# Ten in-projection tiles of a hybrid decoder layer over 516 of 528 positions

## The chip, the cores and the metric

One NeuronCore of a Trainium2 chip runs the whole layer in one launch. The metric is the device time of a launch in microseconds; smaller is better. The engines are named as in the profile: PE is TensorE's matmuls and PEld its weight loads, DVE is VectorE, ACT is ScalarE, POOL is GpSimd, SP is the queue that issues most DMAs.

## The reference

The layer puts 16 learned positions ahead of 512 tokens (528 positions, width 2048, float32), runs a mixer and a feed-forward block, and returns the 512 token positions. The part that matters here:

```python
n = rmsnorm(h, g_pre_mix)                 # (528, 2048)
z = n @ w_in                              # conv: B, C, h (1024 each); rwkv: r, k, v (1024 each), wd, ad (96 each), gd (256)
y_conv = B * causal_dwconv(C * h, conv_w) # kernel of 3 positions
zr = zr + (shift_by_one(zr) - zr) * mu    # token shift of all rwkv columns
r, k, v, wd, ad, gd = split(zr)
log_w = -DECAY_SCALE * sigmoid(w0 + tanh(wd) @ w_decay_up)
a = sigmoid(a0 + ad @ a_up)
g = sigmoid(gd) @ g_up
# S_t = S_{t-1} diag(w_t) + (S_{t-1} a_t) b_t^T + v_t k_t^T ;  y_t = S_t r_t
...
y_rwkv = (group_norm(y) + sum(r * k * r_k) * v) * g
h = h + rmsnorm(concat(y_conv, y_rwkv) @ w_out)
h = h + rmsnorm(conv_glu(rmsnorm(h)))     # conv over 3 positions in the gate
return h[16:]
```

k, v and the decays of a position enter the state and so reach all later positions. r and g of a position enter that position's own output alone. The feed-forward block's convolution looks back two positions, so the mixer's output is needed from position 14 on, and r and g from there, with z one position earlier for the shift.

## The kernel before, in words

Activations lie with channels on the 128 partitions and positions along the free axis. Every large product is done as three products of float32r parts: an operand is split into a rounded part `hi` and a remainder `lo`, and hi*hi, hi*lo and lo*hi are summed in PSUM. A tile of the in-projection is 128 output channels; `inproj` runs `gemm` for it, 16 steps of k (four loads of weights with four steps each), three products, and two halves of the positions, since a PSUM bank holds 512 values: 96 matmuls, each with its own weight load. The halves of the positions are given as a tuple: `HL` is (0, 264), (264, 528), and `HC`, used for two of the three convolution tiles of each group, is (12, 270), (270, 528); `T0` is 14.

There are 52 such tiles: 4 of the LoRAs (decay, a, and two of the gate, called `T_GD` on), 8 each of k, r and v, and 24 for the convolution. `lora_in` does the LoRA's tiles, `rkv(P)` the k, r and v tiles of head pair P, `conv(j)` the convolution's. For an rwkv tile `shifted` calls `inproj` and then `shift`: `evac` multiplies PSUM by the norm's factor into the tile `z` (DVE), ACT copies z times mu into `zm` one position later, with a zero ahead (a POOL memset of one column), and DVE mixes z * (1 - mu) + zm into the output tile (`k`, `r`, `v`, or `tb` for LoRA's). The tail of r, k and v, 16 columns that fill the last chunk of 32 positions, is cleared by a POOL memset ahead of the matmuls.

Head pairs then go through `prep` (which reads r on POOL into `XR`, and on DVE for the bonus), `inverse`, and `scan`, 17 chunks of 32 positions in sequence for each of four groups of four heads; `norm` and, for the last two pairs, `head_norm` finish them. The last pair's output is called `k` again, and its scratch tile `lo` is shared with the product that the last convolution group stores to `ysp`.

The stage is written as generators. A loop of its own time model decides in which order their steps are taken: scans, preps and norms take the steps that are due, and the in-projection tiles fill what is left (k, r, v of the pairs first, then the convolution). The list that results is not yet the order on the engines. `Plan` keeps all operations of the stage with their dependencies, gives each a cost by shape (`Plan.time`; for a matmul below it is n / 2400 + 0.0115 us for n columns), simulates the engines, tries eight rankings and emits the one with the shortest simulated span:

```python
            return max(0.222, n / 600 + 0.004) if x["args"][1].tile.dtype is F32 else n / 2400 + 0.0115
```

In-projection matmuls have the rank `FILL`: PE takes them where nothing else is ready. Each engine's queue then runs in that order. The out-projection follows, first two tiles outside a plan, then the rest and the feed-forward block by Strassen-like sums, under plans of their own. All instructions go through one recording helper, so the profile gives line 231 for them, and tiles' names tell them apart.

Of the kernel before, what the change touches and what calls it, by code (L numbers as in the profile page):

```python
# [12 lines left out]
AF = mybir.ActivationFunctionType  # L13
ALU = mybir.AluOpType
# [7 lines left out]
L = SEQ + META  # L22
# [6 lines left out]
T0 = META - 2  # L29
# [481 lines left out]
def hymba(tc, I, out, ysp=None):  # L511
    nc = tc.nc
    plan = Plan(tc)
    V, S, G, PE, SP = (Engine(plan, n, e) for n, e in (("DVE", nc.vector), ("ACT", nc.scalar), ("POOL", nc.gpsimd),
                                                       ("PE", nc.tensor), ("SP", nc.sync)))
# [19 lines left out]
    def pc(n, i):  # L535
        c = COLS[n] + i
        return par[0][:, c:c + 1] if c < NMIX else par[1][:, c - NMIX:c - NMIX + 1]
# [14 lines left out]
    def gemm(src, mov, spans, first=None, into=None, kept=None, parts=1):  # L552


        for ku in range(KT // 4):
            if kept is not None:
                hi, lo = kept[ku]
            else:
                hi, lo = wload(src[ku], into and into[ku]) if ku or first is None else first
            for k4 in range(4):  # L560
                k = ku * 4 + k4
                ws = slice(k4 * 128, k4 * 128 + 128)
                xh, xl = mov[k]
                for pi, (w, x) in enumerate(((hi, xh), (hi, xl), (lo, xh))):
                    for o, a, b in spans:
                        PE.matmul(o, w[:, ws], x[:, a:b], start=(k == 0 and pi == 0),
                                  stop=(k == KT - 1 and pi == 2))
                    if pi == 2 or parts == 3:
                        yield
# [16 lines left out]
    def split(x, hi, lo, scale=None):  # L586
        if scale is None:
            S.copy(hi, x)
            V.tensor_tensor(out=lo, in0=x, in1=hi.bitcast(F32), op=ALU.subtract)
        else:  # L590
            S.activation(out=hi, in_=x, func=AF.Copy, scale=scale)
            V.scalar_tensor_tensor(out=lo, in0=x, scalar=scale, in1=hi.bitcast(F32), op0=ALU.mult, op1=ALU.subtract)
# [31 lines left out]
    HL = ((0, 264), (264, 528))  # L624
# [3 lines left out]
    with ExitStack() as ctx1:  # L628
# [3 lines left out]
        omu = p1.tile([128, 28 + NP], F32, name="omu")  # L632
# [4 lines left out]
        for i in range(3):  # L637
            t = p1.tile([128, 2, 2, 64], F32, name=f"SUV{i}")
# [9 lines left out]
        for k in range(KT):  # L648
# [3 lines left out]
            if k == 1:  # L652
                SP.dma_start(par[0][:, KT:], I["par"][:, KT:NMIX])
                V.tensor_scalar(out=omu[:, :28], in0=par[0][:, COLS["mu"]:COLS["mu"] + 28], scalar1=-1.0, scalar2=1.0,
                                op0=ALU.mult, op1=ALU.add)
                V.tensor_scalar(out=omu[:, 28:], in0=par[0][:, COLS["k_a"]:COLS["k_a"] + NP], scalar1=-1.0, scalar2=1.0,
                                op0=ALU.mult, op1=ALU.add)
# [20 lines left out]
        def inproj(t, halves, into=None):  # L678
            if t == T_K:

                ps = [stp.tile([128, 512], F32, name="st") for _ in range(2)]
            else:
                ps = mp.tile([128, 2, 512], F32, name="mps")
            yield from gemm(I["w_in"][t], xs, [((ps[i] if isinstance(ps, list) else ps[:, i])[:, :b - a], a, b)
                                               for i, (a, b) in enumerate(halves)],
                            first if t == 0 else None, into, None, 1 if t in (T_WD, T_AD) else PARTS)
            return ps

        def evac(ps, t0, o, halves):

            rstd = norm1[0]
            with plan.step(0.6):
                if not isinstance(ps, list) and halves[0][1] - halves[0][0] == halves[1][1] - halves[1][0]:
                    n = halves[0][1] - halves[0][0]
                    a = halves[0][0]
                    V.tensor_tensor(out=o[:, a - t0:a - t0 + 2 * n].rearrange("p (a b) -> p a b", a=2),
                                    in0=ps[:, :, :n], in1=rstd[:, a:a + 2 * n].rearrange("p (a b) -> p a b", a=2),
                                    op=ALU.mult)
                else:
                    for i, (a, b) in enumerate(halves):  # L700
                        x = ps[i] if isinstance(ps, list) else ps[:, i]
                        V.tensor_tensor(out=o[:, a - t0:b - t0], in0=x[:, :b - a], in1=rstd[:, a:b], op=ALU.mult)

        def shift(ps, mi, o):
            z = p1.tile([128, L], F32, name="z", bufs=2)
            evac(ps, 0, z, HL)
            zm = p1.tile([128, L + 1], F32, name="zm")
            G.memset(zm[:, 0:1], 0.0)
            S.activation(out=zm[:, 1:], in_=z, func=AF.Copy, scale=pc("mu", mi))
            V.scalar_tensor_tensor(out=o, in0=z, scalar=omu[:, mi:mi + 1], in1=zm[:, :L], op0=ALU.mult, op1=ALU.add)  # L710

        def shifted(t, o):
            shift((yield from inproj(t, HL)), t, o)

        blkr = p1.tile([128, 128], F32R, name="blkr")
        blk = p1.tile([128, L], F32, name="lo")[:, :128]
        SP.dma_start(blk, I["cst"][:, 128:256])
# [24 lines left out]
        def lora_in(t):  # L742
            if t == T_WD:
                wad = p1.tile(xr_shape, F32R, name="XR", bufs=2).rearrange("r c a p h t -> r (c a p h t)")
                wd, ad = inproj(t, HL), inproj(T_AD, HL, [
                    (wad[:, 1024 * i:1024 * i + 512], wad[:, 1024 * i + 512:1024 * i + 1024]) for i in range(KT // 4)])
                for _ in range(KT):
                    next(wd)
                    yield
                    if _ >= LAG:  # L750
                        next(ad)
                        yield
                for _ in range(max(0, LAG - LATE)):
                    next(ad)
                    yield
                ps0 = yield from wd
                rstd = p1.tile([128, L], F32, name="rstd")
                m, q = p1.tile([128, LP], F32, name="t1"), p1.tile([128, LP], F32, name="t2")
                for a, b in HL:
                    rms([x[:, a:b] for x in ss], rstd[:, a:b], m[:, a:b], q[:, a:b], aux, "aux")  # L760
                norm1.append(rstd)
                both = p1.tile(xr_shape, F32R, name="XR", bufs=2).rearrange("r c a p h t -> r (c a p h t)")
                lox.extend([both[:, i * L:i * L + L] for i in (2 * n, 2 * n + 1)] for n in range(4))
                tb = p1.tile([128, 2 * C * C + C], F32, name="tb")
                o = tb[:, :L]
                shift(ps0, t, o)
                S.activation(out=o, in_=o, func=AF.Tanh)
                split(o, *lox[0])
                o = tb[:, L:2 * L]
                shift((yield from ad), T_AD, o)  # L770
                split(o, *lox[1])
            else:
                o = p1.tile([128, 2 * C * C + C], F32, name="tb")[:, :L]
                yield from shifted(t, o)
                S.activation(out=o, in_=o, func=AF.Sigmoid)
                split(o, *lox[2 + t - T_GD])

# [34 lines left out]
        def rkv(P):  # L812
            for nm, T in (("k", T_K), ("r", T_R), ("v", T_V)):
                o = p1.tile([128, LP], F32, name=nm, bufs=2)
                G.memset(o[:, L:], 0.0)
                yield from shifted(T + P, o[:, :L])
                st[nm, P] = o

        def prep(P):
# [325 lines left out]
                SP.dma_start(ysp[NP + P], o)  # L1145

        ylast = {}
        HC = ((T0 - 2, T0 - 2 + 258), (T0 + 256, L))

        def conv(j):  # L1150
            zc = p1.tile([128, TY + 2], F32, name="zm")
            evac((yield from inproj(T_CC + j, HC)), T0 - 2, zc, HC)
            zh = p1.tile([128, TY + 2], F32, name="z", bufs=2)
            evac((yield from inproj(T_CH + j, HC)), T0 - 2, zh, HC)
            G.tensor_tensor(out=zc, in0=zc, in1=zh, op=ALU.mult)
# [49 lines left out]
        while tasks or any(fills) or cur:  # L1205
# [4 lines left out]
            if go:  # L1210
                t = min(go, key=lambda t: t[0])
# [46 lines left out]
    with ExitStack() as ctx2:  # L1258
# [132 lines left out]
        for m in range(MS):  # L1391
# [3 lines left out]
            t = mp.tile([128, 2, 512], F32, name="mps")  # L1395
            ps = [t[:, i] for i in range(2)]
# [74 lines left out]
        for n, m in enumerate(range(KT - 2, KT)):  # L1471
            kw = p2.tile([128, KT // 4, 2, 512], F32R, name=f"tt{n}", bufs=1)
            keep = [(kw[:, ku, 0], kw[:, ku, 1]) for ku in range(KT // 4)]
            if n == 0:
                ps = [ps2.tile([128, 512], F32, name="u", bufs=2) for _ in range(2)]
            else:
                t = mp.tile([128, 2, 512], F32, name="mps")
                ps = [t[:, i] for i in range(2)]
# [103 lines left out]
        for b in range(4):  # L1582
            if b % 2 == 0:
                t = p2.tile([128, 2, 2, 1024], F32R, name=f"tt{b // 2}", bufs=1)
# [68 lines left out]
        for f in (2, 3):  # L1653
            t = mp.tile([128, 2, 512], F32, name="mps")
# [3 lines left out]
            for b in (0, 2, 1, 3):  # L1658
# [5 lines left out]
                for _ in fill(standard(outs, w, H * (b % 2), x_of, b % 2 == 0, b % 2 == 1)):  # L1664
                    n += 1
                    if n % 2 == 0:
                        c = next((c for c in chains if c), None)
# [382 lines left out]
```

## Time and profile before

| | us |
|---|---|
| median of three runs | 2360.91 |
| lowest and highest of them | 2359.73, 2362.3 |
| span of the profiled execution, first to last instruction | 2358.4 |
| PE busy in it | 2333.4 |
| PEld, DVE, ACT, POOL busy in it | 2227.5, 1747.5, 1224.2, 631.2 |

For the profiled execution the page gives its span and no separate time; the three timed runs lie 1.3 to 3.9 us above that span, the median 2.5 us.

How to read the rows. In a table of groups a row has the line, engine, operation, output<-inputs and shapes with their count, then busy time and the mean of one in ns, then the idle time ahead of it and who ended that. In the view of one tile a row has the least, median and greatest duration in ns, then the first and last start in us. In a timeline or in the chain of work that ended last, a row starts with the start in us and the length in us, and x gives how many instructions it merges; in brackets stands the idle time of the engine before it and its releaser. Matmuls overlap, and their ends are modelled, so a row's mean duration of a matmul is longer than the distance between two starts.

### The profile page before, as it was taken

What the parts mean: (1) busy time and instruction counts of PE and PEld (TensorE: products, weight loads), DVE (VectorE), ACT (ScalarE), POOL (GpSimd) and SP (SyncE); (2) the same over time, 40 slices, a digit from 0 to 9 for tenths busy, and PEclk for the clock granted to TensorE, in tenths of its full rate; (3) what the DMA queues carried; (4) which work ended last, traced back from release to release, by engine and by line L of the source; (5) the groups of instructions that cost most, each with busy time, mean ns of one, the idle gap of its engine ahead of it and who ended that gap; (6) DMA issues with size and microseconds to landing.
All of it is one profiled execution on the core that took longest, in us unless ns stands there. A gap on an engine that the chain in (4) does not pass through costs nothing.

```text
span 2358.4 us, 46270 instructions
## 1 busy us (share of the span) xinstructions
PE 2333.4 (99%) x18450; PEld 2227.5 (94%) x18450; DVE 1747.5 (74%) x2375; ACT 1224.2 (52%) x2404; POOL 631.2 (27%) x743
## 2 busy tenths in 40 slices
PE   9999999999999999999999999999999999999997
PEld 8999999999999999998989999999999898989897
DVE  7687888878754677785868677776868685959587
ACT  7666766667654556664434344343434352525255
POOL 0231746455351012510112121111212120202024
PEclk9999999999999999999999999999999999999999
DMA  5544332333433755913332324242424242333345
GB/s 184 156 131 120 87 99 85 106 102 104 128 104 90 233 166 170 228 60 108 108 108 88 118 81 135 81 126 80 126 68 138 72 130 86 107 95 96 99 138 116
DMA packets 136583, 274.66 MB, mean 116 GB/s; under 512 B 30992, under 2 KB 50064, under 8 KB 136368
## 3 DMA queue, kind: packets, MB, share of 16 engines
q1 hardware_dynamic: 129584, 265.40, 37.1%
q0 software_dynamic: 6784, 6.31, 1.9%
q8 instruction: 145, 2.38, 0.4%
q14 instruction: 70, 0.57, 0.1%
HBM read 245.82 MB, written 25.84 MB: 115 GB/s over the span
## 4 chain that ended last, share of the span: by engine, by line
PE 96%; DVE 1%; DMA 1%; ACT 1%; issue 0%; POOL 0%; SPq 0%; DVEq 0%; ACTq 0%; POOLq 0%
PE mps L231 60%; PE u L231 18%; PE d L231 11%; PE st L231 4%; PE aux L231 2%; DMA acc<-xT_dram 0%; DMA l<-lo 0%; DVE acc L231 0%; PE psn L231 0%; DVE q L231 0%; DMA r<-xT_dram 0%; DVE wlo L231 0%; POOL acc L231 0%; SPq L231 0%; ACT ahi L231 0%
## 5 line engine op out<-in xcount | busy, mean ns | idle before, releaser
L231 ACT CAST H<-R 128x1024 fp32r<-128x1024 f32 x401 | 420.5, 1050 | 477.6 <-PE u L231 179.5
L231 DVE TENSOR_TENSOR O<-R,H 128x1024 fp32r<-128x1024 f32 x401 | 522.0, 1302 | 121.1 <-ACT H L231 110.6
L231 PE MATMUL mps<-ahi,whi 128*128 128x264 f32 (+2 forms) x1792 | 359.5, 289 | 6.1 <-ACT ahi L231 5.6
L231 PE MATMUL mps<-alo,whi 128*128 128x264 f32 (+2 forms) x1792 | 360.2, 289 | 0.1
L231 PE MATMUL mps<-ahi,wlo 128*128 128x264 f32 (+2 forms) x1792 | 357.8, 288 | 1.2 <-DVE wlo L231 1.0
L231 PE MATMUL mps<-tt,H 128*128 128x258 f32 (+1 forms) x2160 | 287.1, 282 | 1.0 <-ACT q L231 0.9
L231 PEld LDWEIGHTS mps<-ahi,whi 128*128 128x128 f32 x1792 | 273.6, 189 | 8.9 <-ACT ahi L231 5.6
L231 DVE TENSOR_TENSOR wlo<-raw,whi 128x512 fp32r<-128x512 f32 x261 | 198.7, 766 | 106.2 <-ACT whi L231 88.8
L231 PEld LDWEIGHTS mps<-ahi,wlo 128*128 128x128 f32 x1792 | 273.6, 189 | 3.6 <-DVE wlo L231 1.6
L231 PEld LDWEIGHTS mps<-alo,whi 128*128 128x128 f32 x1792 | 273.6, 189 | 3.4 <-DVE alo L231 1.0
L231 PEld LDWEIGHTS mps<-tt,H 128*128 128x128 f32 x2160 | 271.4, 189 | 2.6 <-ACT q L231 1.1
L231 POOL TENSOR_TENSOR raw<-raw,rb 128x514 f32<-128x514 f32 (+2 forms) x45 | 92.8, 2061 | 666.3 <-DVE raw L231 609.8
L231 PE MATMUL mps<-ahi,H 128*128 128x258 f32 (+1 forms) x1064 | 256.7, 282 | 0.0
L231 PE MATMUL mps<-alo,H 128*128 128x258 f32 (+1 forms) x1064 | 256.5, 282 | 0.0
L231 POOL TENSOR_TENSOR R<-R 128x1024 f32<-128x1024 f32 x40 | 132.2, 3304 | 417.6 <-DVE R L231 417.6
L231 ACT CAST whi<-raw 128x512 fp32r<-128x512 f32 x261 | 160.7, 619 | 138.8 <-PE mps L231 85.4
L231 DVE TENSOR_TENSOR R<-R 128x1024 f32<-128x1024 f32 x136 | 226.7, 1667 | 1.9 <-DMA R<-w_pair_dram 0.6
L231 PEld LDWEIGHTS mps<-ahi,H 128*128 128x128 f32 x1064 | 198.3, 189 | 0.0
L231 PEld LDWEIGHTS mps<-alo,H 128*128 128x128 f32 x1064 | 197.9, 189 | 0.0
L231 POOL TENSOR_SCALAR SUV<-VT 32x64 f32<-32x64 f32 x272 | 129.7, 477 | 162.4 <-PE st L231 138.1
L231 PE MATMUL mps<-ahi,O 128*128 128x258 f32 (+1 forms) x1064 | 156.4, 282 | 0.0
L231 PE MATMUL mps<-tt,O 128*128 128x258 f32 (+1 forms) x1080 | 153.1, 281 | 0.0
(339 smaller groups left out, 4576.3 us busy)
## 6 DMA issues: line engine op xcount, KB each, us to landing
R<-w_gu_dram SPq DMA_DIRECT2D x176, 512.0 KB, 3.5
raw<-w_in_dram SPq DMA_DIRECT2D x208, 256.0 KB, 2.7
R<-w_down_dram SPq DMA_DIRECT2D x88, 512.0 KB, 3.8
raw<-w_out_dram SPq DMA_DIRECT2D x32, 256.0 KB, 3.1
R<-w_pair_dram SPq DMA_DIRECT2D x16, 512.0 KB, 4.3
l<-lo SPq DMA_DIRECT2D x24, 264.0 KB, 2.3
out_dram<-acc SPq DMA_DIRECT2D x8, 512.0 KB, 8.5
R<-ysp SPq DMA_DIRECT2D x14, 257.0 KB, 4.5
```

What stands on the lines that cost most here:

```text
L231: return getattr(self.real, op)(*real, **{k: x.get() if isinstance(x, View) else x for k, x in kw.items()})
```

## The change

`shift` and `shifted` take the halves as an argument, with `HL` as its default. The two gate tiles of the LoRA and the eight tiles of r are given `HC`, so the matmuls, the evacuation, the scaled copy and the mix run over positions 12 to 527, 516 instead of 528, in halves of 258. The first of them takes zero for its predecessor. The first 12 columns of the output tile are cleared by a POOL memset, for later steps read all 528. The k, v, decay and a tiles are as they were. `HC` is defined earlier in the function.

```diff
-        def shift(ps, mi, o):
+        def shift(ps, mi, o, halves=HL):
+            c = halves[0][0]
             z = p1.tile([128, L], F32, name="z", bufs=2)
-            evac(ps, 0, z, HL)
+            evac(ps, 0, z, halves)
             zm = p1.tile([128, L + 1], F32, name="zm")
-            G.memset(zm[:, 0:1], 0.0)
-            S.activation(out=zm[:, 1:], in_=z, func=AF.Copy, scale=pc("mu", mi))
-            V.scalar_tensor_tensor(out=o, in0=z, scalar=omu[:, mi:mi + 1], in1=zm[:, :L], op0=ALU.mult, op1=ALU.add)
-
-        def shifted(t, o):
-            shift((yield from inproj(t, HL)), t, o)
-
+            G.memset(zm[:, c:c + 1], 0.0)
+            S.activation(out=zm[:, c + 1:], in_=z[:, c:], func=AF.Copy, scale=pc("mu", mi))
+            if c:
+                G.memset(o[:, :c], 0.0)
+            V.scalar_tensor_tensor(out=o[:, c:], in0=z[:, c:], scalar=omu[:, mi:mi + 1], in1=zm[:, c:L], op0=ALU.mult,
+                                   op1=ALU.add)
+
+        def shifted(t, o, halves=HL):
+            shift((yield from inproj(t, halves)), t, o, halves)
+
+        HC = ((T0 - 2, T0 - 2 + 258), (T0 + 256, L))
...
-                yield from shifted(t, o)
+                yield from shifted(t, o, HC)
                 S.activation(out=o, in_=o, func=AF.Sigmoid)
                 split(o, *lox[2 + t - T_GD])
...
-                yield from shifted(T + P, o[:, :L])
+                yield from shifted(T + P, o[:, :L], HC if nm == "r" else HL)
                 st[nm, P] = o
...
-        HC = ((T0 - 2, T0 - 2 + 258), (T0 + 256, L))
```

## The prediction

> **What bounds the kernel now.** I read the head of the profile page first, then the table of stretches, then the waits of PE, then the chain in order of time. The head of the page:
>
> ```profile
> span 2358.4 us, 46270 instructions
> PE 2333.4 (99%) x18450; PEld 2227.5 (94%) x18450; DVE 1747.5 (74%) x2375; ACT 1224.2 (52%) x2404; POOL 631.2 (27%) x743
> ...
> PE 96%; DVE 1%; DMA 1%; ACT 1%; issue 0%; POOL 0%; SPq 0%; DVEq 0%; ACTq 0%; POOLq 0%
> ```
>
> TensorE is busy for 2333.4 of 2358.4 us and makes up 96% of the chain that ended last. A shorter order of TensorE work therefore shortens the span, as long as it opens no gaps. The stretches (length, then busy time and instructions of PE, PEld, DVE, ACT, POOL, then granted clock and DMA) say where gaps are now:
>
> ```profile
> 0.00:60.00 60.00, 54.19 (x414) 52.74 (x415) 41.50 (x75) 43.48 (x74) 4.58 (x23) 1.00 0.60 188
> 60.00:200.00 140.00, 139.15 (x1228) 137.41 (x1228) 108.55 (x191) 89.17 (x169) 32.92 (x53) 1.00 0.46 141
> 200.00:400.00 200.00, 198.97 (x1933) 189.64 (x1932) 162.36 (x284) 143.35 (x401) 114.89 (x199) 1.00 0.33 94
> 400.00:600.00 200.00, 199.82 (x1951) 190.96 (x1950) 173.92 (x321) 136.39 (x391) 110.25 (x186) 1.00 0.36 103
> 600.00:740.00 140.00, 139.72 (x1289) 133.52 (x1289) 80.50 (x144) 83.68 (x266) 55.40 (x108) 1.00 0.37 110
> 740.00:920.00 180.00, 178.11 (x1477) 177.49 (x1476) 128.05 (x192) 91.26 (x174) 24.31 (x23) 1.00 0.55 169
> 920.00:980.00 60.00, 59.77 (x487) 58.72 (x486) 40.59 (x65) 34.89 (x65) 28.00 (x31) 1.00 0.82 213
> ```
>
> Between 60 and 980 us PE idles for 0.85 + 1.03 + 0.18 + 0.28 + 1.89 + 0.23 = 4.46 us in all; the granted clock is 1.00 throughout. Of PE's waits only the first, at the start of the kernel, is long:
>
> ```profile
> PE mps L231 <- ACT ahi L231: 5.6, 1, 5.6
> PE mps L231 <- DVE wlo L231: 1.0, 1, 1.0
> ```
>
> Where the edited tiles lie is read from the tiles' views, by the VectorE instructions that finish them (mixing in the shifted position):
>
> ```profile
> L231 DVE SCALAR_TENSOR_TENSOR r<-z,omu,zm x8: 754/764/2154, 75.6 to 533.7; 128x528 f32<-128x528 f32 x8
> L231 DVE SCALAR_TENSOR_TENSOR tb<-z,omu,zm x4: 764/769/1218, 44.1 to 159.7; 128x528 f32<-128x528 f32 x4
> L231 POOL MEMSET r<- x8: 106/111/112, 25.9 to 409.4; 128x16 f32 x8
> L231 POOL TENSOR_TENSOR XR<-r,PP x16: 1237/1253/1617, 76.5 to 538.9; 64x544 f32<-64x544 f32 x16
> ```
>
> The eight tiles of r end between 75.6 and 533.7 us, the two of the gate among the four "tb". All sit in the part where PE is full.
>
> **The change part by part.**
>
> *Narrower matmuls.* Each of the ten tiles has 16 steps of k, three products and two halves: 96 matmuls, 960 together, and each goes from 264 columns to 258. Their number and their weight loads stay. The busy time of a matmul does not price this, for it overlaps the next one and shows no gain from 264 columns to 258 (mean ns of one, after the comma):
>
> ```profile
> L231 PE MATMUL mps<-alo,whi 128*128 128x264 f32 x832 | 169.5, 289 | 0.1
> ...
> L231 PE MATMUL mps<-alo,whi 128*128 128x258 f32 x736 | 166.7, 290 | 0.0
> ```
>
> The distance between starts does. In the chain, a long piece of nothing but matmuls divided by its count gives that distance:
>
> ```profile
> 137.18 12.63 PE mps L231 x104
> 173.80 14.06 PE mps L231 x116
> ...
> 761.01 33.54 PE mps L231 x280
> ...
> 1140.05 17.19 PE mps L231 x144
> ...
> 1213.86 5.44 PE u L231 x24
> ```
>
> The first two are in-projection tiles at 264 columns: 26.69 / 220 = 121.3 ns. The third is convolution and out-projection tiles at 258 and 256, in the proportion of these rows of the same stretch:
>
> ```profile
> L231 PE MATMUL mps<-ahi,wlo 128*128 128x258 f32 x67 | 15.0, 283 | 0.0
> ...
> L231 PE MATMUL mps<-ahi,wlo 128*128 128x256 f32 x27 | 7.6, 281 | 0.0
> ```
>
> That is 257.4 columns on the mean at 119.8 ns. From 264 to 257.4 columns the distance falls by 1.5 ns, 0.23 ns a column, so 6 columns are worth 1.4 ns, and 960 x 1.4 = 1.3 us. The far rows give more: the last one is matmuls of 512 columns at 5.44 / 24 = 226.7 ns, the one before it is 144 of the feed-forward block, of 258 and 256 columns again, at 119.4 ns, so 107.3 ns for 255 columns, 0.42 ns a column, 2.5 ns for six, 2.4 us in all. The lower end is nothing, if over this short distance something other than columns sets the pace. I take 1.3 us, from the rows with the same operands and the same neighbours, and keep 0 and 2.4 for the range.
>
> In the Trainium skill, "TensorE: Matmul & The Clock Gate", section "Back-to-back issue gap", an isolated matmul of N columns is put at N / 2.4 + 2.5 ns, so six columns would be an estimated 2.5 ns and 2.4 us, as the far rows say; the same section holds that in a stream of loads and matmuls both together set the distance, and the near rows, with 1.4 ns, lean that way. Its absolute figure for 264 columns, 112.5 ns, is not reached here: the trace has 121.3.
>
> *Shorter evacuation and mixing.* The evacuation, the scaled copy and the mix each lose 12 of 528 elements in ten tiles. The rows of 528 and 516 elements:
>
> ```profile
> L231 DVE TENSOR_TENSOR zm<-mps,rstd x8: 681/695/697, 260.5 to 768.0; 128x516 f32<-128x516 f32 x8
> L231 ACT ACTIVATE zm<-z,parm x28: 722/738/753, 43.2 to 538.8; 128x528 f32<-128x528 f32 x28
> L231 ACT ACTIVATE lo<-zm,parm x8: 721/726/729, 280.6 to 784.2; 128x514 f32<-128x514 f32 x8
> ```
>
> ScalarE falls by some 10 ns a tile (738 to about 727), VectorE by no more than 764 x 12/528 = 17 ns an instruction: 0.1 and at most 0.35 us off engines that are 64 to 87% busy there, beside PE's work. I cost it at nothing.
>
> *Ten memsets more on POOL.* One of 128x12 for each tile; the nearest row, 128x16, has 111 ns, so 1.1 us together. POOL is busy for 115 of the 200 us in the fullest stretch, so they lie in its idle time. Behind such a memset on POOL stand the two products XR<-r of the head pair (1.25 us each), and behind those the scan's operands. If prep of a head pair, not PE, set the end of its stretch, the eight of r would cost 8 x 0.11 = 0.9 us; with 1.5 us of PE idle from 200 to 740 us, over all four scans, it doesn't, so nothing.
>
> *The order.* The planner reckons the in-projection's matmuls 2.5 ns shorter each and lists the whole stage anew, so instructions of all queues may change places. The trace can't show the new list. Bounds: what idling there is can go, −4.46 us, and waits of the same size can come, +4.5. I take 0, because PE always has an in-projection tile to go on with.
>
> Sum: −1.3 + 0 + 0 + 0 against the span of 2358.4, so 2357.1. The runs' median of 2360.91 lies 2.5 us above that span, and with the same distance the time is **2359.6 us**, a change of 0.06%.
>
> **The rivals.**
>
> *Nothing is saved* (0.14). Either the weight load sets the distance, or the saving is lost where the stage ends. For the load: it runs 94% of the span, and the near rows fall less than columns would ask. By the LDWEIGHTS section of the same page of the Trainium skill a load of 128 columns takes 128 / 1.2 = 107 ns, an estimate that would hide matmuls up to 250 columns; no run so far shows a load by itself. Against: 226.7 ns at 512 and 121.3 at 264 are both above 119.8 at 257. For the loss at the end there is the tail of the last head (rows of DVE's timeline, then of ACT's):
>
> ```profile
> 790.56 0.69 DVE L231 TENSOR_TENSOR lo<-lo,z 128x514 f32<-128x514 f32 x1
> ...
> 801.34 0.75 DVE L231 SCALAR_TENSOR_TENSOR k<-al,parm,XR 128x514 f32<-128x514 f32 x1
> ...
> 802.78 0.69 DVE L231 TENSOR_TENSOR alo<-k,ahi 128x514 fp32r<-128x514 f32 x1
> ```
>
> ```profile
> 796.60 0.64 ACT L231 ACTIVATE lo<-Pi 128x528 f32<-128x528 f32 x1 [1.56 <-DMA ysp<-lo]
> ...
> 805.83 0.38 ACT L231 ACTIVATE hxh<-mps 128x258 f32<-128x258 f32 x1
> ```
>
> The last head's output is split by 803.47, and it is the last but one of the 16 steps of k of the first out-projection tile. Two steps of six matmuls, 12 x 0.12 = 1.45 us, lie between its first use and the read of that tile at 805.83: the margin is about 0.9 us. If this chain does not move forward with PE, at most 0.9 us of gain is kept: 2360.0. Against: the chain itself waits at 796.60 for the store of the last convolution group (796.60 <- DMA ysp<-lo), whose last matmuls end just before 790, so it does move with PE. In either case 2360.0 to 2360.9.
>
> *Slower: the tail comes late* (0.13). The same chain, put off by the new list: each microsecond of lateness beyond 0.9 us is a PE wait of one, since the terms before it are done by then. It is slower by over 0.2% (4.7 us, about what a measurement of this kernel can tell from no change) from a lateness of 4.7 + 1.3 + 0.9 = 6.9 us, and gives 2365.6 or more. For: the chain has a DMA, two engines in turn and a split in a row, with 0.9 us to spare. Against: such a lateness is nearly eight times that margin, and the matmuls of the second out-projection tile can be done meanwhile.
>
> *Faster by more than 0.2%* (0.15). The new list takes out waits: 4.7 − 1.3 = 3.4 of the 4.46 us of idle, or with 2.4 us for the matmuls 2.3 of them; 2354.0 to 2356.2. For: 1.89 us of the idle is in one stretch, 740 to 920, and 5.8 us more at the start. Against: the start hangs on the first loads, which the change doesn't touch, and the stretches from 400 on hold almost nothing to recover.
>
> **How the numbers follow.** The forecast, with 0 to 2.4 us saved and up to 1.5 us of new or lost idle, has 0.58 and its own range is 2357.0 to 2361.5. With the case of nothing saved, 0.58 + 0.14 = 0.72 for within 0.2%; 0.15 for faster and 0.13 for slower. The range from 2355.5 to 2365.5 leaves out the far half of the faster case and nearly all of the slower one, just under 0.2.
>
> **What would show it.** In the changed profile the tiles of r and of the gate have matmuls of 258 columns, 960 fewer at 264; long pieces of the chain with them stand at 119.5 to 120.2 ns a matmul instead of 121.3. The r-mix has 516 elements, and there are ten memsets of 128x12 on POOL with no wait behind them that reaches PE. PE's busy time falls by 1 to 2.4 us and its idle from 60 to 980 us stays between 3 and 6 us; the out-projection's first evacuation, at 805.83 now, comes 1 to 2.4 us earlier. The forecast is wrong if that evacuation is earlier by over 4 us or later than now, or if a new PE wait of microseconds stands behind ACT or DVE in the scans or at the tail.

## The result and the profile after

The changed kernel takes 2364.39 us (median; 2361.7 to 2366.16) against 2360.32 us before: 4.1 us more, ratio 1.0016 with a 95% interval of 1.001 to 1.0021. The forecast was 2359.6, a gain. The head of the page after:

```profile
span 2362.2 us, 46287 instructions
PE 2334.6 (99%) x18450; PEld 2229.0 (94%) x18450; DVE 1746.1 (74%) x2375; ACT 1225.2 (52%) x2404; POOL 639.6 (27%) x753
...
PE 95%; DVE 2%; DMA 1%; ACT 1%; issue 0%; SPq 0%; POOL 0%; DVEq 0%; ACTq 0%
```

The edit is there as planned. The view of the tile r shows 516 elements and eight memsets of 128x12 (two more stand in the view of `tb`, the gate's), and POOL has 753 instructions instead of 743. After:

```profile
L231 POOL MEMSET r<- x16: 102/110/116, 25.5 to 409.1; 128x16 f32 x8, 128x12 f32 x8
...
L231 DVE SCALAR_TENSOR_TENSOR r<-z,omu,zm x8: 702/752/757, 75.0 to 538.0; 128x516 f32<-128x516 f32 x8
```

TensorE has the same 18450 matmuls, 960 of them narrower, and is yet busy for 1.2 us longer. The table of stretches after:

```profile
60.00:200.00 140.00, 139.43 (x1234) 137.84 (x1233) 104.42 (x191) 90.30 (x172) 33.33 (x56) 1.00 0.47 140
200.00:400.00 200.00, 199.00 (x1934) 189.39 (x1933) 160.70 (x285) 143.52 (x399) 113.81 (x204) 1.00 0.32 93
400.00:600.00 200.00, 197.09 (x1917) 187.67 (x1916) 166.10 (x304) 132.40 (x376) 110.86 (x179) 1.00 0.35 102
600.00:740.00 140.00, 139.22 (x1286) 132.80 (x1286) 86.51 (x152) 82.43 (x265) 64.45 (x114) 1.00 0.38 111
740.00:920.00 180.00, 178.08 (x1479) 177.26 (x1478) 129.35 (x195) 94.42 (x185) 22.74 (x22) 1.00 0.54 169
920.00:980.00 60.00, 59.81 (x490) 58.97 (x489) 42.17 (x66) 34.93 (x66) 26.85 (x29) 1.00 0.75 203
```

PE idles for 0.57 + 1.00 + 2.91 + 0.78 + 1.92 + 0.19 = 7.37 us from 60 to 980 us, where it was 4.46. Most of the difference is between 400 and 600 us: 2.91 for 0.18. The waits of PE say for whom:

```profile
PE mps L231 <- ACT ahi L231: 5.6, 1, 5.6
PE mps L231 <- DVE wlo L231: 2.5, 4, 1.1
PE mps L231 <- ACT q L231: 0.9, 1, 0.9
PE mps L231 <- DVE zm L231: 0.8, 1, 0.8
PE st L231 <- POOL s L231: 0.7, 1, 0.7
```

The first and third stand in the list of before too. New are longer waits for remainders of weights (wlo), one for an evacuation (zm), and one for the scan's scaled state (s). The evacuation stands on DVE behind work that waited for a DMA, and PE waits for it (DVE's timeline, then PE's):

```profile
636.81 0.77 DVE L231 SCALAR_TENSOR_TENSOR sg<-sg,parm,lo 128x528 f32<-128x528 f32 x1 [1.76 <-DMA lo<-l]
...
640.48 0.69 DVE L231 TENSOR_TENSOR zm<-mps,rstd 128x516 f32<-128x516 f32 x1
```

```profile
641.32 0.47 PE L231 MATMUL mps<-ahi,whi 128*128 128x258 f32 x2 [0.78 <-DVE zm L231]
```

The out-projection's first evacuation starts at 808.83, 3.0 us later than before; the prediction had named a later start as a sign of being wrong.

That leaves part of the difference past the mixer. Each operation of DVE, ACT and POOL from 1010 us on has the same place in its queue in both kernels, so their starts can be set side by side: the changed kernel is 2.4 us later at 1100 us, 3.1 at 1700 and 3.8 at 2300. The feed-forward block, which the edit doesn't touch, takes 1.45 us more, evenly spread.

### The profile page after: what moved, and what is told of

Same layout as the page of the kernel before. It is cut to its first block, busy times and chain, and to the rows that moved or that the text cites. A ratio compares the mean times of both kernels' runs of the same rounds, so it can differ in the third digit from the quotient of the medians.

```text
span 2362.2 us, 46287 instructions
## 1 busy us (share of the span) xinstructions
PE 2334.6 (99%) x18450; PEld 2229.0 (94%) x18450; DVE 1746.1 (74%) x2375; ACT 1225.2 (52%) x2404; POOL 639.6 (27%) x753
## 4 chain that ended last, share of the span: by engine, by line
PE 95%; DVE 2%; DMA 1%; ACT 1%; issue 0%; SPq 0%; POOL 0%; DVEq 0%; ACTq 0%
PE mps L231 60%; PE u L231 18%; PE d L231 11%; PE st L231 4%; PE aux L231 2%; DVE wlo L231 0%; DVE acc L231 0%; DMA raw<-w_in_dram 0%; DMA d<-tb 0%; PE psn L231 0%; DVE q L231 0%; DMA lo<-l 0%; DMA l<-lo 0%; DMA acc<-xT_dram 0%; DVE tt L231 0%
## 5 line engine op out<-in xcount | busy, mean ns | idle before, releaser
L231 ACT CAST H<-R 128x1024 fp32r<-128x1024 f32 x401 | 420.4, 1050 | 478.0 <-PE u L231 179.4
L231 DVE TENSOR_TENSOR O<-R,H 128x1024 fp32r<-128x1024 f32 x401 | 522.3, 1303 | 121.8 <-ACT H L231 111.8
L231 PE MATMUL mps<-ahi,whi 128*128 128x258 f32 (+2 forms) x1792 | 359.3, 288 | 6.5 <-ACT ahi L231 5.6
L231 PE MATMUL mps<-alo,whi 128*128 128x258 f32 (+2 forms) x1792 | 361.1, 289 | 0.0
L231 PE MATMUL mps<-ahi,wlo 128*128 128x258 f32 (+2 forms) x1792 | 356.9, 288 | 2.5 <-DVE wlo L231 2.5
L231 POOL TENSOR_SCALAR SUV<-VT 32x64 f32<-32x64 f32 x272 | 134.8, 496 | 147.8 <-PE st L231 124.3
```

The source lines that it names most:

```text
L231: return getattr(self.real, op)(*real, **{k: x.get() if isinstance(x, View) else x for k, x in kw.items()})
```

## The experiments

Theory 1 was that the list costs the time: other prices give another order of the whole first stage. Theory 2 was that the work does, by the memsets or the narrower tiles themselves. For the first two runs the planner's prices were tied to the tile, so that the work of one kernel runs in the order of the other; in their traces PE, DVE, ACT and POOL take all instructions but the memsets in exactly that order. In what follows, a run is compared with the kernel before as timed beside it (2360.17 to 2360.47 us in the three sets).

**Narrow tiles in the old order.** The edit, in `Plan.time`: the PSUM and `z` tiles of the ten carry a mark `pad`, and what reads or writes them is priced as if it were wide.

```diff
+        if e == "POOL" and op == "memset" and n == T0 - 2:
+            return 0.0
+        if any(isinstance(a, View) and getattr(a.tile, "pad", 0) for a in [out] + x["ins"]):
+            n += 6 if e == "PE" else 12
```

> The ten tiles at 516 positions and with their memsets, as in the change, but priced by the planner as if they were wide, so that every engine's queue has the order of the kernel before (POOL has the ten memsets more). Theory 1 (the new list costs the time): 1.2 to 2.4 us below before, about 2359 us beside 2360.3. Theory 2 (the memsets or the narrower tiles themselves cost it): near the changed kernel, 2363 to 2365 us, with a PE idle of 7 us from 60 to 980 us instead of 4.5.

Measured: 2359.11 us against 2360.47, ratio 0.9996 (0.9987 to 1.0005). That agrees with the forecast's 1.3 us, though the interval doesn't part it from no change. Its stretches, to the one at 600 us:

```profile
60.00:200.00 140.00, 138.35 (x1223) 136.44 (x1222) 106.88 (x189) 89.05 (x168) 33.43 (x56) 1.00 0.46 141
200.00:400.00 200.00, 198.74 (x1936) 189.47 (x1935) 162.15 (x285) 142.62 (x400) 113.50 (x200) 1.00 0.33 94
400.00:600.00 200.00, 199.83 (x1952) 190.95 (x1951) 174.00 (x321) 136.56 (x391) 111.25 (x188) 1.00 0.35 102
```

Of the changed kernel's 2.9 us of idle between 400 and 600, 0.17 are left, with the memsets and the narrow tiles in place. From 60 to 200 us it idles for 1.65 us, where the kernel before has 0.85, so that from 60 to 980 us it has 5.5 us for 4.46. The profiled execution (2360.86 us) is the slowest of the eleven, so such sums of single traces are a guide only. From 1010 us to the end it runs at a constant distance to the kernel before, to 0.01 us. Theory 2 is out: what the work itself does is the small gain.

**Wide matmuls in the new order.** The matmuls and the evacuation of the ten tiles run over `HL` again, and the planner takes the 6 and 12 off, `n -= 6 if e == "PE" else 12` in the same place.

```diff
-            evac(ps, 0, z, halves)
+            evac(ps, 0, z, HL)
...
-            shift((yield from inproj(t, halves)), t, o, halves)
+            shift((yield from inproj(t, HL)), t, o, halves)
```

> The matmuls and the evacuation of the ten tiles over all 528 positions, everything else as in the change, priced by the planner as if narrow, so that every queue has the order of the changed kernel. Theory 1 (list): 1.2 to 2.4 us above the changed kernel, 2365.5 to 2367 us. Theory 2 (work): near before, 2360 to 2362 us. The feed-forward block, 1.45 us longer in the changed kernel's trace, stays long if that goes with the list, and is as before if it goes with the ten tiles' work.

Measured: 2365.0 us, ratio 1.0019 (1.001 to 1.0028), 0.6 us over the changed kernel, less than the 1.2 to 2.4 that were expected. The loss comes with the list and without the edit's work, and the feed-forward block is as long as in the changed kernel. So both parts of the loss go with the list.

**Other lists for the same work.** One number of the planner changed, in the kernel before:

```diff
-            return max(0.222, n / 600 + 0.004) if x["args"][1].tile.dtype is F32 else n / 2400 + 0.0115
+            return max(0.222, n / 600 + 0.004) if x["args"][1].tile.dtype is F32 else n / 2400 + 0.0113
```

> The kernel before with one number of the planner changed: a matmul is priced at n/2400 + 0.0113 us instead of 0.0115, on all tiles alike. The work is the same, the list of the first stage is another. Theory 1: the time moves by some us either way, 2357 to 2366, and mostly up. Theory 2: no change, within 0.5 us of before.

> As the run with 0.0113, with 0.0117. Theory 1: another list, another time, 2357 to 2366 us, and unlike the 0.0113 run by a microsecond or more. Theory 2: within 0.5 us of before.

Measured: 2360.97 us (ratio 1.0005, 0.9996 to 1.0014) and 2362.84 us (1.0012, 1.0003 to 1.002). The first looks like no change and is not: in its trace the feed-forward block is 1.55 us shorter than before, and what comes ahead of it is longer by about as much. In the second the block is 1.55 us shorter as well, so its lists cost 3.9 us. This price also redoes later plans (the orders differ from the kernel before's up to 1050 us, in the changed kernel up to 761); from there on they are the same.

**Where tiles lie.** The instructions of the feed-forward block are the same in both kernels, and so are the operands' names. What differs is where six of the 32 tiles of split activations lie: ahi5, ahi10, ahi11, alo4, alo9 and alo10. A tile gets its place in SBUF when the list first names it, and the list now names these in another order. Two runs swap the places and leave the lists, a third gives the narrow tiles the places of a third layout, all by one line ahead of the stage's emission:

```diff
+        for n in "0 1 0' 2 1' 3 2' 3' 4 4' 5 5' 6 6' 7 7' 8 8' 9 9' 10 11 10' 11' 12 12' 13 13' 14 14' 15 15'".split():
+            xs[int(n.rstrip("'"))][n.endswith("'")].tile.get()
         plan.give()
```

(The order shown is that of the kernel before. The changed kernel's has 4 5 4' 5' and 9 10 9' 10' 11 11', the third has 10 10' 11 11', so that it differs from the kernel before by one exchange of two neighbours, alo10 and ahi11.)

> The changed kernel with every queue in its own order, but the 32 tiles of split activations (ahi, alo) laid out in SBUF as in the kernel before; six of them lie elsewhere in the changed kernel, since a tile gets its place when the list first names it. Theory of places: the feed-forward block, 1.45 us longer in the changed kernel from 1010 to 2320 us at the same instructions, falls back by 1.4 to 1.5 us, and the time by about that, to 2363 us. Rival, that the longer block comes from when its transfers and other engines' work fall: no change, 2364.4 us.

> The kernel before, its lists untouched, with the 32 tiles laid out as in the changed kernel. Theory of places: the feed-forward block 1.4 to 1.5 us longer, about 2361.9 us in all. Rival: 2360.4 us.

> The narrow tiles in the order of the kernel before (2359.1 us), with the 32 tiles laid out as in the kernel before that was priced with 0.0113, whose feed-forward block was 1.55 us shorter. If the places of these tiles alone decide, 1.5 us less, about 2357.6 us; if those of the weight buffers, which differ there too, share in it, anything from 2357.5 to 2359.5 us. Theory of the rival: no change.

Measured: 2362.88 us (ratio 1.0009, 1.0 to 1.0018), 2361.72 us (1.0005, 0.9996 to 1.0014) and 2357.19 us (0.9986, 0.9977 to 0.9994). The block's length is read off the chain of work that ended last: two pieces of 144 matmuls, the same instructions in each kernel, one near the start of the block and one near its end. Kernel before (the start's row, 1140.05, stands in the prediction), changed kernel, new list with old places, old list with new places, narrow tiles with the third places:

```profile
2272.58 17.19 PE mps L231 x144
```

```profile
1142.48 17.21 PE mps L231 x144
...
2276.38 17.21 PE mps L231 x144
```

```profile
1141.25 17.19 PE mps L231 x144
...
2273.78 17.19 PE mps L231 x144
```

```profile
1139.90 17.21 PE mps L231 x144
...
2273.79 17.21 PE mps L231 x144
```

```profile
1139.04 17.16 PE mps L231 x144
...
2270.09 17.16 PE mps L231 x144
```

From row to row that is 1132.53, 1133.90, 1132.53, 1133.89 and 1131.05 us. In the four runs of two lists and two layouts the length follows the places to 0.01 us and does not care for the list. In the third layout, one exchange away, it is 1.48 us shorter than before; that kernel, the narrow tiles in the old order with the third places, is the fastest here, 3.0 us below the kernel before and 7.2 below the change.

**One of the new waits.** In the changed kernel two products on POOL run beside two remainders of weights (`wlo`) on DVE, and PE waits for the first of them (POOL's timeline, then DVE's, then PE's):

```profile
529.43 4.21 POOL L231 TENSOR_TENSOR XR<-XR,PC 64x1024 f32<-64x1024 f32 x2
```

```profile
529.76 4.43 DVE L231 TENSOR_TENSOR wlo<-raw,whi 128x512 fp32r<-128x512 f32 x2
```

```profile
531.93 0.50 PE L231 MATMUL mps<-ahi,wlo 128*128 128x258 f32 x2 [1.07 <-DVE wlo L231]
```

The kernel before has such pairs too. POOL runs two of these products from 249.3 to 253.5 us, and a remainder on DVE takes 1.76 us there, where its median is 0.69:

```profile
252.30 1.76 DVE L231 TENSOR_TENSOR wlo<-raw,whi 128x512 fp32r<-128x512 f32 x1
```

But from 250 to 300 us PE has no wait at all in the kernel before. What is new is not that the two run together, but that PE is already in need of the remainder. The run leaves the two products out of the changed kernel:

```diff
                 G.tensor_tensor(out=xd, in0=xd, in1=PC[q, p, :NC - 1]...
+                if P == 6:
+                    plan.kept[-1]["drop"] = True
...
             for x in self.order():
+                if "drop" in x:
+                    continue
```

> The changed kernel with its lists, without the two products XR<-XR,PC of head pair 6 on POOL (so that pair's chunks are not scaled by the decay): they run from 529.4 to 533.6 us there, two DVE remainders of weights beside them take 4.4 us instead of 1.4, and PE waits 1.23 us at 530.6. Theory (the new list lays a POOL product beside a remainder that PE needs): the remainders take 0.7 us each, PE's wait at 530.6 is gone, and the time falls by 0.8 to 1.3 us, to about 2363.3. Rival (PE would have waited there for the cast on ACT or the load in any case, or the gain is lost later in the scan): 2364.2 to 2364.6 us.

Measured: 2361.86 us, 2.5 us below the changed kernel, more than the 0.8 to 1.3 that were expected. DVE's row at that place and PE's wait for remainders there:

```profile
530.72 1.28 DVE L231 TENSOR_TENSOR wlo<-raw,whi 128x512 fp32r<-128x512 f32 x2
```

```profile
PE mps L231 <- DVE wlo L231: 1.2, 2, 1.1
```

The two remainders take 1.28 us for 4.43, and two of the four waits for wlo are gone (the 1.1 us that is left is a wait past 800 us). Set beside the changed kernel's trace, this run is 0.96 us later at 520 us (the two executions differ by that since the first loads) and 0.22 us earlier at 533, a step of 1.2 us as expected. It gains 0.95 us more in three smaller steps by 710, which were not expected: without the products POOL is also free 4.2 us sooner, and what of that brings these steps was not taken apart. The gain stays to the last instruction: nothing later in this run gives the wait back.

In the Trainium skill, "SBUF — State Buffer", section "SBUF: two separate sides", DVE operations with two SBUF inputs and GpSimd operations that read SBUF take turns on one pair of ports, the later one blocked for the whole of the other. These rows agree: 4.43 us beside the product, 1.28 without it.

**What a matmul's columns are worth.** The prediction had two slopes, 0.23 and 0.42 ns a column, and a floor that could not be seen. In the old order, with the planner priced as for 264:

```diff
                     for o, a, b in spans:
+                        if o.tile.__dict__.get("pad") and (k or pi):
+                            o, b = o[:, :240], a + 240
```

> As narrow_old_list (2359.1 us), every queue in the order of the kernel before, but of the 96 matmuls of each of the ten tiles 94 run over the first 240 of the 258 columns of their half, 18 fewer (the last 18 columns of each half keep only their first product), 940 matmuls in all. If columns set the distance as between 257 and 512 columns, 0.42 ns each: 940 x 18 x 0.42 = 7.1 us less, 2352 us. If by the 0.23 ns a column of the prediction's near rows: 3.9 us less, 2355.2. If the weight load sets the distance: 2359.

> The same with 216 of 258 columns, 42 fewer on 940 matmuls. By 0.42 ns a column 16.6 us less, 2342.5 us; by 0.23 ns 9.1 us less, 2350; by the load alone, or if PE then waits for other engines, no less than in the run at 240 columns.

Measured: 2354.99 us (ratio 0.9979, 0.997 to 0.9989) and 2356.04 us (0.9983, 0.9974 to 0.9992). The time at 240 columns is 4.1 us below that at 258, as the smaller slope said, but not for its reason. At 216 columns it falls no further. One piece of the chain of 104 matmuls, 68 of them of a gate tile, is the same in the old list at four widths; it stands as 137.18 12.63 at 264 columns in the prediction, and here at 258, 240 and 216:

```profile
138.39 12.57 PE mps L231 x104
```

```profile
135.91 12.04 PE mps L231 x104
```

```profile
135.78 11.98 PE mps L231 x104
```

Shared over the 68 matmuls the steps are 0.06 / 68 = 0.9 ns from 264 to 258 columns, 0.53 / 68 = 7.8 ns from 258 to 240, and 0.06 / 68 = 0.9 ns from 240 to 216. The whole first stage says the same: the mean distance of two starts of equal width from 60 to 740 us, those over 140 ns left out, is 121.6 ns at 264, 120.2 at 258, 112.3 at 240 and 109.1 at 216. So the curve is flatter over the six columns of the change, steep from there to 240, and flat again below. Two things are mixed in. The step from 264 to 258 also moves the columns at which the halves begin, from 0 and 264 to 12 and 270, where the later steps leave them; the two were not parted. And at 216 columns the untouched matmuls of 264 stand 123.0 ns apart on the mean, for 121.8 at 240 and 121.7 at 258. That takes back part of what the narrow ones gain, and why is open. Of the 7.4 us that 940 x 7.9 ns would give at 240 columns, part turns into waits: in the old order, made for wider tiles, PE idles for 4.9 us from 60 to 400 us there, and for 2.9 with 258 columns.

In the Trainium skill, "TensorE: Matmul & The Clock Gate", section "LDWEIGHTS (loading the stationary operand)", a load of 128 columns takes 128 / 1.2, an estimated 107 ns; a level of 109 to 112 ns agrees with a load for each matmul. No run here takes the loads away, so that the load makes this level is not shown.

**Is it this list or any list?** The changed kernel with other prices, which again reach into later plans, and with the old places:

> The changed kernel with matmuls priced at n/2400 + 0.0113 us, so with another list of the first stage again, and with the 32 tiles of activations laid out as before. If a new list costs 2 to 4 us over the old one whatever it is made for, 2361 to 2363 us; if the loss belongs to the one list of the change, about 2359 us, the time of the narrow tiles in the old list.

> The same with 0.0117. If any new list costs 2 to 4 us, 2361 to 2363 us and not the same as with 0.0113; if the loss belongs to the change's own list, about 2359 us.

Measured: 2364.91 us (ratio 1.0021, 1.0011 to 1.003) and 2366.45 us (1.0028, 1.0018 to 1.0038), above the 2 to 4 us that were expected. With the narrow tiles and the old places there are now four lists: the old one 2359.1, the change's 2362.9, and these. PE's idle from 60 to 980 us rises with them in the traces: 5.5, 7.3, 8.8 and 10.1 us. None of the five new lists tried, for either width, is as good as the old one once the feed-forward block's length is taken out. Whether some other would be was not tried.

## Why the prediction was wrong

The change of 4.1 us comes apart by the medians of the runs (the kernel before moved by 0.3 us between the sets): narrow tiles in the old order −1.2 (2360.32 to 2359.11), their new list +3.8 (to 2362.88), the places that the list gives to tiles +1.5 (to 2364.39).

- *Narrower matmuls, −1.3 us.* Borne out as far as it can be told: 1.2 to 1.4 us by the medians (with an interval that includes no change), 1.4 ns a matmul by the distances. The near rows were a better guide than the far ones with their 2.4 us, since they lie on the same flatter piece of the curve: 1.4 ns from 264 to 258 is 0.23 ns a column, where it is 0.42 from 512 to 264 and 0.44 from 258 to 240.
- *Evacuation and memsets, nothing.* No loss shows: with both in place the old order is not slower than before.
- *The order, 0 because PE always has an in-projection tile to go on with.* This is the step that failed: the new list costs 3.8 us. A tile to go on with needs its weights' remainder from DVE and a free PSUM buffer from an evacuation, and the scans need POOL. The new list lays a POOL product beside a remainder that PE needs at once (529.4 us), and an evacuation (`zm`) behind instructions that wait for a DMA, and PE waits for each: 7.37 us of idle for 4.46. Of the list's 3.8 us the idle explains 1.9 (7.3 us for 5.5, narrow tiles and old places in both) to 2.9, as far as single traces tell; the rest was not taken apart. The 3.8 us lie inside the bounds of ±4.5 us, but the upper one was set equal to the lower without a reason, and the middle was wrong: the old list had little idle to lose, and none of the five new ones was as good.
- *What was not in the sum.* That a new list also gives tiles other places, and that these change the pace of 1.3 ms of matmuls elsewhere: +1.5 us. No step of the prediction speaks of a cost in the feed-forward block.
- *The rival of the late tail.* The side was right, the place and the size were not: it asked for 2365.6 us or more by a wait at the tail. From 740 to 920 us PE idles for 1.92 us, 1.89 before; the waits are in the scans.
- *The rival of the load.* The distance does level off, near 110 ns, but below 240 columns; from 264 to 258 it still falls.

## What to carry to other kernels

Where a planner orders instructions from modelled costs, an edit that touches a cost can buy a new order of a whole stage. Here that cost 3.8 us for a gain of 1.3. Time the edit's work in the old order first, by pricing it as it was, then the new order with the old work; the two together say which of them to keep. Where addresses follow from the order of first use, pin them, or a comparison of two orders is also one of two layouts. And a single trace shows which waits are there; their sum says less than the medians of many runs.

## What the runs showed of the hardware that was not expected

The places of six tiles in SBUF change the time of identical matmuls. From 1120 to 2290 us a matmul of 256 or 258 columns starts 0.2 to 0.3 ns later on the mean after the one ahead of it in the changed kernel, by tile in both directions: behind a matmul that reads ahi11 at 256 columns the distance goes from 116.7 to 120.0 ns, behind ahi10 from 117.9 to 117.1. Matmuls whose own tile stays where it was change too: behind one that reads ahi8 at 256 columns it goes from 115.8 to 117.5. At 512 columns there is no loss (226.9 and 226.7 ns). Three layouts of the same tiles span 2.85 us in 1132. Which property of an address does this stays open. The distance also doesn't fall evenly with the columns: 0.9 to 1.4 ns for six columns below 264, some 8 ns for the next 18, 1 to 3 ns for the next 24.
